# Mixer's output projection: three steps prepared during the last gates, its weight sums in the norm rows' room, and bank copies ahead of casts

## The chip, the cores and the metric

The kernel runs on one core of a Trainium2 chip. The metric is the device time of one execution in microseconds (us), median of several runs. The engines of the core run side by side, each in its own order: PE (TensorE: matmuls, and PEld its weight loads), DVE (VectorE), ACT (ScalarE), POOL (GpSimd) and SP (SyncE, which here issues all loads).

## The reference

Two layers of an encoder on a sequence of 512 tokens with 1024 channels, float32. Each layer has three sandwich-normalised blocks: a SwiGLU feed-forward (FFN1), a mixer, and a second feed-forward (FFN2).

```python
h = rms_norm(x, norm_pre[l, 0])
x = x + 0.5 * rms_norm(swiglu_ffn(h, ...), norm_post[l, 0])
h = rms_norm(x, norm_pre[l, 1])
m = hybrid_mixer(h, w_in[l], ..., w_branch[l], w_out[l])
x = x + rms_norm(m, norm_post[l, 1])
h = rms_norm(x, norm_pre[l, 2])
x = x + 0.5 * rms_norm(swiglu_ffn(h, ...), norm_post[l, 2])
```

The end of the mixer is what the change touches:

```python
branches = jnp.stack([sb_out, conv_out, gla_out], axis=2)      # each 512 x 512
branch_d = jnp.einsum('bsgw,gwd->bsgd', branches, w_branch)
gates = jax.nn.sigmoid(gate_logits.reshape(b, s, N_BRANCHES, D_MODEL))
merged = jnp.sum(gates * branch_d, axis=2)
return merged @ w_out
```

## The kernel before, in words

**Split products.** Every float32 operand of a matmul is split into a high part (a cast to the matmul's short float32 form, on ACT) and a low part (raw minus high, on DVE). Each product is three matmuls: high x high, high x low, low x high. A weight load of 128 x 1024 thus costs one cast (`whi`) and one subtraction (`wlo`). There are five buffers for such pairs, and three raw buffers of two halves each (`load_raw`), into which SP loads. Line 115/116 is the general `split`; lines 676, 677, 679 and 680 are the same for the output projections (`Down.parts`).

**Order.** A planner lays out each engine's instructions at build time. Instructions made with `pinned` (`keep_in_program_order`) stand behind everything that the program text has put on that engine before them; the others may be moved, and buffers of a kind are handed out as the plan goes. All matmuls are pinned.

**Gates.** `gates(g, src, done)` handles one branch g in eight steps d of 128 output channels. A step computes the gate logits (24 matmuls, bank `gate`), their sigmoid `gs` on ACT, the branch's projection (12 matmuls, bank `pb`), then the product of the two on DVE (line 1222) and the sum into `acc[d]` on POOL (line 1223). The branches come in the order 0, 2, 1; the last is the convolution's (`cv`), and only there `done` is given (`merge`). Before the change each step loads its own gate weights at its start.

**The output projection.** `merged @ w_out` has its first half (`acc[0..3]`, 512 of the 1024 inner channels) done as a block product with seven smaller products in place of eight (class `Down`, after Strassen and Winograd), and the other half (`acc[4..7]`) as ordinary products. A step p of the list `steps` is one product. `sums(p)` loads its weights and forms the sums of weights and of tokens on DVE (lines 642 and 662), `parts(p)` splits them into high and low parts, `product(p)` runs twelve matmuls into the banks oA, oB, oC or oD. `ahead()` does `sums` of the next step and `parts` of this one. The mixer has `PER` = 1 (one product per kind), the FFNs have 4. So the mixer's list is: steps 0 to 5 and 6 (the seven products), then steps 7 to 10 (`acc[4..7]`), whose matmuls run token block by token block in `out_proj`.

Four steps are prepared before the first product. Before the change one of them is prepared in gate step 6 of the last branch (`merge`), the others in `run` after the gates. `run` takes the room of the activations, xh, for the weight sums (`kept`), and xl for copies (`taps`) of banks that are used again. In the loop of `run` the preparation of a later step (`ahead`) comes first and the copy of a bank (line 720) after it.

**Norm rows.** Each block needs the norm's weight rows, one before and one after it, broadcast to 128 x 1024 (`load_g`, line 193, tag `g`, two buffers). An FFN loads them in `run` (`late`, after the products of kind 3); the mixer before its start.

Of the kernel before, what the change touches and what calls it, by code (L numbers as in the profile page):

```python
# [8 lines left out]
F32 = mybir.dt.float32  # L9
# [4 lines left out]
P = 128  # L14
D = 1024
S = 512
NT = S // P
KC = D // P
# [19 lines left out]
C_GQ, C_GK, C_GV, C_GR, C_LR, C_GATE = 2560, 2816, 3072, 3584, 4096, 4112  # L38
# [3 lines left out]
def kernel(  # L42
# [17 lines left out]
    gp = ctx.enter_context(tc.tile_pool(name="gp", bufs=2))  # L60
# [15 lines left out]
    def bank(n, tag="pb"):  # L76
        return psp.tile([P, 512], F32, tag=tag, name=n, bufs=BANKS[tag])
# [23 lines left out]
    def room(n, dt=F32R):  # L101
        cur[n] = resid.tile([P, KC, S], dt, tag=n, name=n)
        return cur[n]
# [47 lines left out]
    def proj_cols(w2d, c0, name, tag="pb"):  # L151
        wh, wl = load_cols(w2d, c0)
        ps = bank(name, tag)
        mm_cols(ps, wh, wl)
        return ps
# [140 lines left out]
    def mm_out(o, t, sh, sl, wh, wl, st=False, en=False):  # L296
        mm(o, sh[:, t], wh, start=st, stop=False, skip_group_check=True)
        mm(o, sh[:, t], wl, start=False, stop=False, skip_group_check=True)
        mm(o, sl[:, t], wh, start=False, stop=en, skip_group_check=True)
# [271 lines left out]
    class Down:  # L571
# [6 lines left out]
        def __init__(self, wd, hid, f0, np, middle, last):  # L578
            self.wd, self.hid = wd, hid
            self.F0, self.NP, self.PER = f0, np, np // 2  # L580
            self.MIDDLE, self.LAST = middle, last
            self.ready = {}
            self.s1 = None
            self.next = 0
            self.raw = {}
            self.plan()
# [36 lines left out]
        def load(self, p):  # L623
# [8 lines left out]
                                       self.wd[r0:r0 + 2 * P, HS[h]].rearrange("(k p) c -> p k c", p=P))]))  # L632
            self.raw[p] = raws

        def sums(self, p):

            self.load(p)
            j, c = self.steps[p]
            if j is None:
                return  # L640
            name, raws = self.ORDER[j][0], self.raw[p]
            tt = lambda o, a, b, op: pinned(nc.vector.tensor_tensor(o, a, b, op=op))
            kept = last = None
            if j >= 2:

                at = lambda n: self.kept[:, n:n + 2, :].rearrange("p k c -> p (k c)")
                last = at(2 * c)
                kept = at(2) if self.PER == 1 and j > 2 else last
            src = raws[0]
            if name == "S3":  # L650
                tt(kept, raws[0], raws[1], ALU.subtract)
                src = kept
            if name == "S2":
                for q, x in enumerate(self.of(p)):
                    tt(x, self.s1[c][:, q], x, ALU.add)
                tt(kept, last, raws[0], ALU.subtract)
                src = kept
            if name == "S4":
                for q, x in enumerate(self.of(p)):
                    tt(x, x, self.hid[self.F0 + 2 * c + q][:, self.R1], ALU.add)  # L660
            if name == "S1":
                pinned(nc.vector.scalar_tensor_tensor(src, kept, -1.0, raws[0], op0=ALU.mult, op1=ALU.subtract))
            if name == "A22":
                tt(src, kept, raws[0], ALU.add)
            self.raw[p] = src
# [43 lines left out]
        def run(self, late, order=("C0", "D0", "C1", "D1", "B0", "B1")):  # L709
            got = {n: bank("o" + n[0]) for n in order}  # L710
            c0, d0, c1, d1, b0, b1 = (got[n] for n in ("C0", "D0", "C1", "D1", "B0", "B1"))
            a0, a1 = (bank("oA", "pa") for i in range(2))
            self.banks = {"A": (a0, a1), "B": (b0, b1), "C": (c0, c1), "D": (d0, d1)}
            self.out = [[c0, d0], [c1, d1], [b0, a0], [b1, a1]]
            self.kept, taps = room("xh", F32), room("xl", F32)
            p1, p7, self.u2, self.u4 = ([taps[:, n + i, :] for i in range(2)] for n in (0, 2, 4, 6))

            def tap(o, b):
                for i in range(2):
                    pinned(nc.scalar.copy(o[i], self.banks[b][i]))  # L720

            while self.next < self.AHEAD:
                self.ahead()
            for p in range(self.end):
                j, c = self.steps[p]
                self.product(p)
                self.ahead()
                if c != self.PER - 1:
                    continue
                if j == 1:  # L730
                    tap(p1, "A")
                if j == 2:
                    tap(p7, "C")
                if j == 3:
                    tap(self.u2, "A")
                    late()
                if j == 5:
                    tap(self.u4, "A")
                    for i in range(2):
                        pinned(nc.vector.tensor_tensor(self.u4[i], p7[i], self.u4[i], op=ALU.subtract))  # L740

                    self.p1 = [slot("p1") for i in range(2)]
                    for i in range(2):
                        pinned(nc.scalar.copy(self.p1[i], p1[i]))
                    if not self.MIDDLE:

                        sh, sl, hi, lo = self.ready[self.end]
                        for i in range(2):
                            mm_out(self.out[i][1], slice(i * P, (i + 1) * P), sh, sl, hi[:, HS[1]], lo[:, HS[1]], st=True)
            while self.next < len(self.steps):  # L750
                self.ahead()
            rest = []
            for p in range(self.end, len(self.steps)):
                sh, sl, hi, lo = self.ready[p]
                rest.append((self.steps[p][1], (hi, lo), (sh, sl)))
            return self.out, rest, None if self.MIDDLE else self.LAST[0]
# [106 lines left out]
        return out_proj(wd, NF, None, TAIL, lambda i, b: finish(i, b, down.sum), upcoming, early, head)  # L863


    def mixer(l, wv, arrive, finish, upcoming, early):
        W = w_in[l]

        NR = TAPS + 3
# [136 lines left out]
        taps = []  # L1006
# [178 lines left out]

        acc = [None] * KC

        def gate_branch(g, d, src, wb):
            pg = proj_cols(W, C_GATE + g * D + d * P, "gate")
            sg = slot("gs", tag="s")  # L1190
            nc.scalar.activation(sg, pg, AF.Sigmoid)
            pb = bank("pb")
            wh, wl = wb
            for k in range(4):
                sh, sl = src[k]
                mm(pb, wh[:, k, :], sh, start=(k == 0), stop=False)
                mm(pb, wh[:, k, :], sl, start=False, stop=False)
                mm(pb, wl[:, k, :], sh, start=False, stop=(k == 3))
            return pb, sg
# [11 lines left out]
            return r  # L1211

        def gates(g, src, done):
            for d in range(0, KC, 2):
                wb = load_branch(g, d)
                for dd in (d, d + 1):
                    pb, sg = gate_branch(g, dd, src, wb[dd - d])
                    if acc[dd] is None:
                        acc[dd] = slot("acc", tag="q")
                        nc.vector.tensor_tensor(acc[dd], pb, sg, op=ALU.mult)  # L1220
                    else:
                        nc.vector.tensor_tensor(sg, pb, sg, op=ALU.mult)
                        nc.gpsimd.tensor_tensor(acc[dd], acc[dd], sg, op=ALU.add)
                    if done is not None:
                        done(dd)
                    yield
# [136 lines left out]
        def merge(d):  # L1363
            for n in range(2):
                down.sum_tokens(d, n)
            if d == KC - 2:
                down.ahead()

        for _ in gates(1, cv, merge):
            pass  # L1370
        head = down.run(lambda: None, ("B0", "B1", "C0", "C1", "D0", "D1"))
        return out_proj(w_out[l], KC, None, TAIL, lambda i, b: finish(i, b, down.sum), upcoming, early, head)


# [14 lines left out]
    weights = None  # L1389
    subs = [(l, s) for l in range(L) for s in range(3)]  # L1390
    for idx, (l, s) in enumerate(subs):
        norms = []

        def late():
            norms.append(load_g(norm_post[l, s]))
            if idx + 1 < len(subs):
                norms.append(load_g(norm_pre[subs[idx + 1][0], subs[idx + 1][1]]))

        if s == 1:
            late()  # L1400
        upcoming = []
        here, forms = forms, Forms() if s != 0 else None
        ahead = forms
# [19 lines left out]
        if s == 0:  # L1423
            weights = ffn(f1g[l], f1u[l], f1d[l], weights, here, arrive, finish, upcoming, early, late,
                          begin if idx == 0 else None)
        elif s == 1:
            weights = mixer(l, weights, arrive, finish, upcoming, early)
        else:
            weights = ffn(f2g[l], f2u[l], f2d[l], weights, here, arrive, finish, upcoming, early, late, None)
        arrive = upcoming  # L1430
# [29 lines left out]
```

## Time and profile before

| | |
|---|---|
| median of 3 runs | 2356.39 us (2355.69 to 2358.6) |
| profiled execution, its own time | 2358.0 us |
| its span, first to last instruction | 2356.3 us |
| mean granted TensorE clock | 0.994 |
| PE busy | 2315.5 us (98%) |
| DVE busy | 1887.7 us (80%) |
| ACT busy | 1240.8 us (53%) |
| POOL busy | 162.6 us (7%) |

The profile is one execution of the program. Its views used here are: the totals per engine; the chain of work that ended last (followed back from the last instruction to what released each step); windows, which give for a stretch of time the busy time and count of an engine, the granted TensorE clock and the load of the DMA engines; the timeline, one row per instruction with its start, its duration, engine, line, operation, output and inputs, and in brackets the idle time of the engine before it with what ended it; waits, which add such idle times up; and tiles, which show all instructions on one buffer name. Matmul durations overlap, since matmuls are pipelined; what counts is the distance from one start to the next.

### The profile page before, as it was taken

The page shows a single profiled execution, that of the slowest core. Times are in us where ns is not written, and L with a number is a line of the kernel's source. Part 1 is how long each engine was busy: PE and PEld are TensorE (multiplying, and loading weights), DVE is VectorE, ACT ScalarE, POOL GpSimd, SP SyncE. Part 2 cuts the span into 40 slices and gives each one's busy share as a digit, 9 for nine tenths or more (in the row PEclk, how much of TensorE's full clock was granted, in tenths as well). Part 3 has the DMA queues.
Part 4 walks back from the last instruction along what each step waited for, and adds up shares of the span by engine and source line. Part 5 has one row for each costly group of instructions (what it writes and reads, how often), then busy time and mean ns, then how long its engine had stood idle before and what let it go on. Part 6 is the DMA issues. An engine that isn't in the chain of part 4 may idle for free.

```text
span 2356.3 us, 36269 instructions
## 1 busy us (share of the span) xinstructions
PE 2315.5 (98%) x14048; PEld 2059.4 (87%) x14048; DVE 1887.7 (80%) x2819; ACT 1240.8 (53%) x2414; POOL 162.6 (7%) x277
## 2 busy tenths in 40 slices
PE   8999999999999899999999999999999998999998
PEld 7999888887888689998899998888878886999987
DVE  7888987859964688889888889877699637888897
ACT  5565656633322455556555566665433324655664
POOL 0000001201021000000000000022010210000000
PEclk9999999999999899999999999999999999999999
DMA  5333644141332323336423336532223323233363
GB/s 172 95 103 108 231 144 118 54 113 48 101 104 90 109 69 101 108 108 215 161 78 102 108 113 229 159 100 72 77 72 95 102 72 116 73 108 108 108 223 108
DMA packets 335965, 269.53 MB, mean 114 GB/s; under 512 B 12874, under 2 KB 285292, under 8 KB 335792
## 3 DMA queue, kind: packets, MB, share of 16 engines
q1 hardware_dynamic: 335792, 267.21, 37.4%
q8 instruction: 110, 1.80, 0.3%
q14 instruction: 63, 0.52, 0.1%
HBM read 265.07 MB, written 2.10 MB: 113 GB/s over the span
## 4 chain that ended last, share of the span: by engine, by line
PE 94%; DVE 3%; ACT 1%; issue 1%; DMA 0%; POOL 0%; SPq 0%; DVEq 0%; POOLq 0%; ACTq 0%
PE A L66 19%; PE gate L66 11%; PE oA L66 10%; PE C L66 9%; PE oC L66 6%; PE pb L66 5%; PE B L66 5%; PE oB L66 3%; PE pf L66 3%; PE gr L66 2%; PE pa L66 2%; PE q L66 2%; PE gv L66 2%; PE pv L66 2%; PE pgl L66 2%; PE k L66 2%
## 5 line engine op out<-in xcount | busy, mean ns | idle before, releaser
L457 DVE TENSOR_TENSOR wlo<-raw,whi 128x1024 fp32r<-128x1024 f32 (+1 forms) x304 | 331.2, 1089 | 108.4 <-ACT whi L455 107.6
L455 ACT CAST whi<-raw 128x512 fp32r<-128x512 f32 x532 | 315.3, 620 | 162.7 <-DVE raw L457 162.7
L115 ACT CAST whi<-raw 128x1024 fp32r<-128x1024 f32 (+1 forms) x162 | 168.1, 1044 | 323.1 <-PE gate L66 134.6
L116 DVE TENSOR_TENSOR wlo<-raw,whi 128x1024 fp32r<-128x1024 f32 (+1 forms) x162 | 203.6, 1266 | 134.0 <-ACT whi L115 129.8
L457 DVE TENSOR_TENSOR raw<-raw 128x512 f32<-128x512 f32 x304 | 209.3, 689 | 5.7
L66 PE MATMUL A<-xh,whi 128*128 128x256 f32 x608 | 172.5, 284 | 0.0
L66 PE MATMUL A<-xl,whi 128*128 128x256 f32 x608 | 172.0, 283 | 0.0
L66 PE MATMUL A<-xh,wlo 128*128 128x256 f32 x608 | 172.0, 283 | 0.0
L1042 DVE SCALAR_TENSOR_TENSOR y<-u,cw,y 128x511 f32<-128x511 f32 (+14 forms) x240 | 166.7, 756 | 0.0
L680 DVE TENSOR_TENSOR wlo<-raw,whi 128x1024 fp32r<-128x1024 f32 x122 | 149.3, 1223 | 18.4 <-ACT whi L677 18.4
L677 ACT CAST whi<-raw 128x1024 fp32r<-128x1024 f32 x122 | 128.4, 1052 | 64.8 <-issue 19.6
L66 PE MATMUL gate<-xh,wlo 128*128 128x512 f32 x384 | 152.3, 397 | 8.5 <-DVE wlo L116 8.5
L66 PE MATMUL gate<-xh,whi 128*128 128x512 f32 x384 | 153.4, 400 | 1.0 <-ACT whi L115 1.0
L66 PE MATMUL gate<-xl,whi 128*128 128x512 f32 x384 | 151.3, 394 | 0.0
L66 PE MATMUL oA<-whi,dh 128*128 128x512 f32 x352 | 139.2, 395 | 5.1 <-ACT xl L720 5.1
L66 PE MATMUL oA<-wlo,dh 128*128 128x512 f32 x352 | 140.0, 398 | 3.9 <-DVE wlo L680 3.9
L66 PE MATMUL oA<-whi,dl 128*128 128x512 f32 x352 | 138.7, 394 | 0.0
L268 POOL TENSOR_TENSOR rs<-ms,mhalf 128x1 f32<-128x1 f32 x44 | 25.1, 576 | 1453.6 <-DVE ms L266 1453.6
L455 ACT COPY cp<-A 128x256 f32<-128x256 f32 x228 | 84.4, 370 | 68.3 <-PE A L66 67.4
L66 PEld LDWEIGHTS A<-xl,whi 128*128 128x128 f32 x608 | 116.5, 192 | 0.2
L66 PEld LDWEIGHTS A<-xh,whi 128*128 128x128 f32 x608 | 116.4, 191 | 0.2
L66 PEld LDWEIGHTS A<-xh,wlo 128*128 128x128 f32 x608 | 116.5, 192 | 0.0
(324 smaller groups left out, 7088.9 us busy)
## 6 DMA issues: line engine op xcount, KB each, us to landing
raw<-in_ffn_w_down_dram SPq DMA_DIRECT2D x152, 512.0 KB, 4.6
raw<-in_w_in_dram SPq DMA_DIRECT2D x108, 512.0 KB, 4.5
raw<-in_ffn_w_gate_dram SPq DMA_DIRECT2D x152, 256.0 KB, 3.4
raw<-in_ffn_w_up_dram SPq DMA_DIRECT2D x152, 256.0 KB, 4.5
raw<-in_w_branch_dram SPq DMA_DIRECT2D x24, 512.0 KB, 3.7
raw<-in_w_out_dram SPq DMA_DIRECT2D x24, 512.0 KB, 4.7
raw<-in_ffn_w_gate_dram SPq DMA_DIRECT2D x12, 512.0 KB, 5.7
raw<-in_ffn_w_up_dram SPq DMA_DIRECT2D x12, 512.0 KB, 5.3
```

The costliest lines, as they stand in the source:

```text
L66: tc.keep_in_program_order(nc.tensor.matmul(*a, **k))
L115: pin(nc.scalar.copy(hi, src))
L116: pin(nc.vector.tensor_tensor(lo, src, hi.bitcast(F32), op=ALU.subtract))
L268: nc.gpsimd.tensor_tensor(self.rs, ms, mhalf[:, 0:1], op=ALU.pow)
L455: copy = lambda o, i: pin(nc.scalar.copy(o, i))
L457: tt = lambda o, a, b, op: pin(nc.vector.tensor_tensor(o, a, b, op=op))
L677: pinned(nc.scalar.copy(hi, src))
L680: pinned(nc.vector.tensor_tensor(lo, src, hi.bitcast(F32), op=ALU.subtract))
L1042: nc.vector.scalar_tensor_tensor(y[:, back:], u[:, :S - back], cw[:, c, j:j + 1], y[:, back:], op0=ALU.mult, op1=ALU.add)
```

## The change

1. In the last branch's `gates` the gate weights of step d + 1 are loaded before the matmuls of step d (`following`), those of step 0 before the branch's first weights.
2. `merge` prepares three steps of the output projection (`ahead` three times) in gate step 6, where it prepared one.
3. In the mixer the weight sums get two buffers of the tag `g` (`apart`) instead of the room of xh. The mixer's norm rows use the same two buffers, and are loaded by `late` after product 3 instead of before the mixer.
4. In the mixer's `run` the copies of banks, `late`, the early matmuls of step 7 and the difference for `u4` stand ahead of `ahead`; in the FFNs the order stays.

```diff
@@ class Down
-            self.s1 = None
+            self.s1 = self.apart = None
...
+        def place(self, n):
+            return self.kept[:, n:n + 2, :].rearrange("p k c -> p (k c)")
@@ Down.sums
-                at = lambda n: self.kept[:, n:n + 2, :].rearrange("p k c -> p (k c)")
-                last = at(2 * c)
-                kept = at(2) if self.PER == 1 and j > 2 else last
+                if self.PER == 1 and not self.apart:
+                    self.apart = [gp.tile([P, D], F32, tag="g", name="kept") for n in range(2)]
+                if self.PER > 1:
+                    last = kept = self.place(2 * c)
+                else:
+                    last, kept = self.apart[0], self.apart[min(j - 2, 1)]
@@ Down.run
-            self.kept, taps = room("xh", F32), room("xl", F32)
+            if self.PER > 1:
+                self.kept = room("xh", F32)
+            taps = room("xl", F32)
...
                 self.product(p)
-                self.ahead()
+                if self.PER > 1:
+                    self.ahead()
...
                         for i in range(2):
                             mm_out(self.out[i][1], slice(i * P, (i + 1) * P), sh, sl, hi[:, HS[1]], lo[:, HS[1]], st=True)
+                if self.PER == 1:
+
+                    self.ahead()
@@ mixer
-    def mixer(l, wv, arrive, finish, upcoming, early):
+    def mixer(l, wv, arrive, finish, upcoming, early, late):
...
-        def gate_branch(g, d, src, wb):
-            pg = proj_cols(W, C_GATE + g * D + d * P, "gate")
+        def gate_weights(g, d):
+            return load_cols(W, C_GATE + g * D + d * P)
+
+        def gate_branch(g, d, src, wb, w):
+            pg = bank("gate")
+            mm_cols(pg, *w)
...
         def gates(g, src, done):
+
+            early_ = done is not None
+            following = gate_weights(g, 0) if early_ else None
             for d in range(0, KC, 2):
                 wb = load_branch(g, d)
                 for dd in (d, d + 1):
-                    pb, sg = gate_branch(g, dd, src, wb[dd - d])
+                    w = following if early_ else gate_weights(g, dd)
+                    if early_ and dd + 1 < KC:
+                        following = gate_weights(g, dd + 1)
+                    pb, sg = gate_branch(g, dd, src, wb[dd - d], w)
...
             if d == KC - 2:
-                down.ahead()
+                for n in range(3):
+                    down.ahead()
...
-        head = down.run(lambda: None, ("B0", "B1", "C0", "C1", "D0", "D1"))
+        head = down.run(late, ("B0", "B1", "C0", "C1", "D0", "D1"))
@@ the layers' loop
-        if s == 1:
-            late()
...
-            weights = mixer(l, weights, arrive, finish, upcoming, early)
+            weights = mixer(l, weights, arrive, finish, upcoming, early, late)
```

## The prediction

> **What bounds the kernel now.** I read the page first: engine totals, the clock row, the chain.
>
> ```profile
> span 2356.3 us, 36269 instructions
> PE 2315.5 (98%) x14048; PEld 2059.4 (87%) x14048; DVE 1887.7 (80%) x2819; ACT 1240.8 (53%) x2414; POOL 162.6 (7%) x277
> PE 94%; DVE 3%; ACT 1%; issue 1%; DMA 0%; POOL 0%; SPq 0%; DVEq 0%; POOLq 0%; ACTq 0%
> ```
>
> TensorE (PE) sets the time: 94% of the chain lies on it, and it is idle for only about 41 us. The change adds and removes no matmul, so it can win only where PE waits or runs at a lower clock. Then I looked for those places with the chain and with windows around the mixer's end (columns of a window: length, PE busy and count, granted clock, DMA share, GB/s).
>
> ```profile
> 766.71 5.44 PE gate L66 x24
> 774.71:814.71 40.00, 31.74 (x110) 0.83 0.37 124
> 1943.62:1982.85 39.23, 29.68 (x110) 0.87 0.38 127
> 814.71:833.75 19.04, 19.04 (x85) 1.00 0.35 100
> ```
>
> The first row (chain of waits) is one undisturbed gate: 24 matmuls in 5.44 us, 0.2267 us each. The next two are the place that the change touches, once per layer: from where gate 7 of the last branch could start to the first matmul into bank oD. The program has 36 matmuls of gate 7 there and 72 of six block products, 108 in all (the window counts 110, with those on its edges). At 0.2267 us they need 24.48 us. They take 40.00 and 39.23, at a clock of 0.83 and 0.87; behind them it is 1.00. The loss is 15.52 + 14.75 = **30.27 us**, the most that this change can win there. The timeline of PE in both layers shows where it goes (start, us, and in brackets the idle time before it and who ended it):
>
> ```profile
> 774.48 0.39 PE L66 MATMUL pb<-brh,wlo 128*128 128x512 f32 x1
> 775.39 0.50 PE L66 MATMUL gate<-xh,whi 128*128 128x512 f32 x1 [0.52 <-ACT whi L115]
> 779.74 0.79 PE L66 MATMUL gate<-xh,wlo 128*128 128x512 f32 x1 [3.61 <-DVE wlo L116]
> 780.33 0.63 PE L66 MATMUL gate<-xh,whi 128*128 128x512 f32 x1
> 790.41 0.39 PE L66 MATMUL oB<-whi,dh 128*128 128x512 f32 x1
> 795.47 0.50 PE L66 MATMUL oA<-wlo,dh 128*128 128x512 f32 x1 [1.95 <-DVE wlo L680]
> 804.77 0.50 PE L66 MATMUL oA<-whi,dh 128*128 128x512 f32 x1 [2.19 <-ACT xl L720]
> 806.67 0.63 PE L66 MATMUL oA<-wlo,dh 128*128 128x512 f32 x1
> 814.71 0.39 PE L66 MATMUL oD<-whi,dh 128*128 128x512 f32 x1
> 1944.30 0.50 PE L66 MATMUL gate<-xh,whi 128*128 128x512 f32 x1 [0.52 <-ACT whi L115]
> 1948.64 0.80 PE L66 MATMUL gate<-xh,wlo 128*128 128x512 f32 x1 [3.61 <-DVE wlo L116]
> 1958.60 0.39 PE L66 MATMUL oB<-whi,dh 128*128 128x512 f32 x1
> 1963.66 0.50 PE L66 MATMUL oA<-wlo,dh 128*128 128x512 f32 x1 [1.95 <-DVE wlo L680]
> 1964.22 0.40 PE L66 MATMUL oA<-whi,dh 128*128 128x512 f32 x1
> 1967.27 0.50 PE L66 MATMUL oC<-wlo,dh 128*128 128x512 f32 x1 [0.58 <-DVE wlo L680]
> 1972.95 0.50 PE L66 MATMUL oA<-whi,dh 128*128 128x512 f32 x1 [2.89 <-ACT xl L720]
> ```
>
> Three stalls. Gate 7 waits for its own weights; without that wait oB would start at 774.71 + 36 x 0.2267 = 782.87 instead of 790.41 (7.54 us), in layer 1 at 1951.78 instead of 1958.60 (6.82). The second product waits for its low weight part, the fourth for a copy out of bank A. Together PE idles 8.27 us in layer 0 and 9.55 in layer 1; the other 7.3 and 5.2 of the loss are matmuls of 0.63 instead of 0.39 us, and restarts, behind the stalls (780.33, 806.67).
>
> **The change part by part.** The reason of the first stall stands in ACT's and DVE's order:
>
> ```profile
> 750.20 1.06 ACT L115 CAST whi<-raw 128x1024 fp32r<-128x1024 f32 x1 [1.17 <-PE pb L66]
> 772.25 0.60 ACT L1191 ACTIVATE gs<-gate 128x512 f32<-128x512 f32 x1 [7.56 <-PE gate L66]
> 772.74 0.70 ACT L676 CAST dh<-acc 128x256 fp32r<-128x256 f32 x2
> 773.35 1.05 ACT L677 CAST whi<-raw 128x1024 fp32r<-128x1024 f32 x1
> 774.29 1.04 ACT L115 CAST whi<-raw 128x1024 fp32r<-128x1024 f32 x1
> 774.98 0.69 DVE L1222 TENSOR_TENSOR gs<-pb,gs 128x512 f32<-128x512 f32 x1 [7.47 <-PE pb L66]
> 775.59 1.82 DVE L679 TENSOR_TENSOR dl<-acc,dh 128x256 fp32r<-128x256 f32 x2
> 775.81 1.31 POOL L1223 TENSOR_TENSOR acc<-acc,gs 128x512 f32<-128x512 f32 x1 [6.87 <-DVE gs L1222]
> 777.33 1.21 DVE L680 TENSOR_TENSOR wlo<-raw,whi 128x1024 fp32r<-128x1024 f32 x1
> 778.47 1.21 DVE L116 TENSOR_TENSOR wlo<-raw,whi 128x1024 fp32r<-128x1024 f32 x1
> 797.14 0.75 DVE L679 TENSOR_TENSOR dl<-acc,dh 128x256 fp32r<-128x256 f32 x2
> 804.14 1.07 ACT L720 COPY xl<-oA 128x512 f32<-128x512 f32 x2
> ```
>
> *Gate weights one gate ahead.* Nothing is added, two loads and splits change places. Gate 6's weights are cast at 750.20, 16 us before gate 6 starts. Gate 7's (L115 at 774.29) stand behind the pinned casts of step 0, and those behind gate 6's sigmoid. Loaded before gate 6, they come ahead of step 0, in the buffer that gate 4 leaves some 19 us before gate 7 starts (two gates of 8.16, and the 12 branch matmuls of gate 4, 2.72). The first stall goes: 7.54 + 6.82 us. What is late next is the products' preparation.
>
> *Three steps prepared in the last gate but one.* Same instructions, earlier. What held steps 1 and 2 back: the sums went into the room of xh, which gate 7 still reads.
>
> ```profile
> SPq L127 <- DVE xh L642: 75.1, 2, 37.9
> raw<-in_w_out_dram SPq DMA_DIRECT2D x24, 512.0 KB, 4.7
> DMA to landing us min/median/max: 3.5/4.5/5.5
> ```
>
> Even the load queue stood 37.9 us per layer for a sum in xh. With the sums in the norm rows' room, DVE runs on from 775.59 (from start to start: weight low 777.33 to 778.47, 1.14 us; a weight sum is of the same size, 1.13; a pair of token lows 0.67 of its 0.75, and 1.74 beside POOL's add). Step 0 is ready at 778.5, the sum and lows of step 1 at 781.4, the two token sums, the weight sum and lows of step 2 at 785.0. Then gate 7's multiply (0.61), and with sum and lows at about 3.0 us each, step 3 at 788.6, step 4 at 791.5, step 5 at 793.9 and step 6 at 795.7. PE, without a stall, starts product 0 at 782.87 and each next 12 x 0.2267 = 2.72 us later: 785.59, 788.31, 791.03, 793.75, 796.47; six matmuls into oD at 799.19, product 6 at 800.55. Every step is ready 2.2 us or more ahead, and this is the cover. POOL's add for gate 7 will stretch one low by 1.1 us (1.74 against 0.67), which the cover holds; without it the 1.1 us would stand on PE, once per layer. Raw weights: step 4's come into the raw buffer that step 0 and gate 7 shared, free at 778.5, and land 4.7 us later, at 783.3, for a sum at 785.6.
>
> On this stretching the Trainium skill ("Advanced Engine Details and Errata", Mode Summary) says that VectorE's second SBUF port is shared with GpSimd and that the two block each other. By it all of the moved DVE work that runs beside POOL's adds would slow down, at most 1.3 us per add; the two rows above (1.82 beside POOL, 0.75 without) agree, and the sum is the same by either.
>
> *Bank copies ahead of casts.* The fourth product waited for a copy (804.14) that stood behind casts waiting for DVE sums. Now the copy of bank A needs product 1's end (788.5) and is done at 789.5, for product 3 at 791.03. The reverse price: the casts of steps 5, 7 and 9 wait for copies. For step 9 that means: copy of A from 798.7 (its first half is whole 9 matmuls into product 5), a second pair of copies behind it (together 2.2 us), casts of steps 9 and 10 from 800.9, the low of step 10 ends at 805.45. PE reads it 10 matmuls and 8 weight parts into the first token, at 805.5. I take 0.4 us per layer for this, between 0 and 1.8 us (the whole chain of cast and low, 0.52 + 1.22, late).
>
> *Norm rows late.* Two 512 KB loads per layer leave the mixer's start and come behind product 3, their rooms free at 785 (low of step 2) and 790 (sum of step 5).
>
> ```profile
> SPq L193 <- DVE tn L272: 13.5, 2, 6.8
> 822.43 0.69 DVE L272 SCALAR_TENSOR_TENSOR tn<-xl,g 128x512 f32<-128x512 f32 x1
> ```
>
> At the mixer's start the queue no longer stands 6.8 us per layer; no PE wait lies there, so nothing is won. At the end they land by 790 + 5.5 = 795.5; first use is at 822.43 - 15.5 = 806.9: hidden by 11 us. Step 8's load may stand behind them on SP until 790 and land at 795 to 796.5; its cast is due at 796.5. Without cover it would hold up the copies of bank A behind it, about 1 us; counted in the 1.8.
>
> **Sum.** Against the profiled execution (2358.0 us, span 2356.3): -30.3 + 0.8 = -29.5, so 2328.5. The median, 2356.39, is 1.6 below that execution; I forecast 2356.4 - 29.5 = **2327** (likeliest case alone: 2324 to 2331).
>
> **The rivals.**
> - *Only the gate stall goes.* DVE has some 20 us of work from 775.6 to the low of step 6, in 25 us of PE work. If loads or POOL put it more than 2.2 us behind, waits come back at products 3 to 5, with the slow clock. Gain 7.54 + 6.82 = 14.4: **2342**. For it: the margins are one instruction wide. Against: they are worked from measured starts.
> - *The slow clock stays.* The part of the loss that is not idle time is 7.3 + 5.2 = 12.5 us. Were the slow runs periodic and not caused by the stalls, it would stay: 2327 + 12.5, **2339**. Against it: the windows before and after have clock 1.00. By the Trainium skill ("TensorE: Matmul & The Clock Gate", Why this matters for your kernels) only idle gaps over some 3 us throw the clock back. The trace differs: slow rows (806.67) follow a gap of 2.19 us, and in layer 1 the row at 1964.22 shows full speed behind one of 1.95; the measurement decides.
> - *Nothing changes.* The buffers decide: five for split weights, fourteen small slots, of which eight hold the last branch's splits until gate 7 ends. If steps 1 and 2 get theirs only then, the same work comes at the same time and gate 7's weights lie behind it: **2356**. Against: step 0 to 2 need six slots and gate 6's sigmoid one, and the fifteenth comes free at 777.1, with POOL's add.
> - *Slower: the gates starve.* One more gate's weights are held in the same five buffers. If in the last group each gate's cast starts only when the gate before leaves a buffer, cast and low (1.05 + 1.21) stand on PE, with 1.6 us of slow clock (8 matmuls): 3.9 us for each of 14 gates, 54 against 30: **2380**. It decides from 8 such gates on. Against: weights are cast 16 us ahead now, two gates.
>
> **How the numbers follow.** Forecast 0.70; gate stall only 0.13; slow clock stays 0.04; nothing 0.06; slower 0.07. 0.2% is 4.7 us, about what a measurement of this kernel can tell from no change. Faster: 0.87, same 0.06, slower 0.07. The range holds the forecast, the slow clock and the better half of the gate case: 2323 to 2342.
>
> **What would show it.** Windows like the two above: 108 matmuls in 24.5 to 26 us at clock 1.00; no wait of a gate for L116; the casts of steps 0 to 2 all behind gate 6's sigmoid and ahead of gate 7's; the xl copy of bank A ahead of step 5's cast; the norm rows' loads near product 3. I am wrong if products wait for L680 or L720 again, if gates 1 to 6 of the last group wait, or if the token stage starts with a wait.

## The result and the profile after

| | before | after |
|---|---|---|
| median of 4 runs | 2356.51 us (2355.69 to 2358.6) | 2327.96 us (2327.32 to 2329.25) |
| profiled execution, its own time | 2358.0 us | 2327.66 us |
| its span | 2356.3 us | 2325.9 us |
| mean granted TensorE clock | 0.994 | 0.999 |

The ratio is 0.9878, 95% interval [0.9861, 0.9895]: the changed kernel is 28.6 us faster, where 2327 us was forecast. The totals and the chain of the page after:

```profile
PE 2302.7 (99%) x14048; PEld 2052.4 (88%) x14048; DVE 1884.8 (81%) x2819; ACT 1240.1 (53%) x2414; POOL 176.8 (8%) x277
PE 96%; DVE 2%; ACT 1%; issue 0%; DMA 0%; POOL 0%; SPq 0%; DVEq 0%; POOLq 0%; ACTq 0%
```

PE does the same 14048 matmuls. Its busy time falls by 12.8 us (2315.5 to 2302.7), nearly all of it at the two places of the change, where the slow matmuls are gone (31.74 + 29.68 us before, twice 24.48 after). The rest of the 30.4 us of span is idle time. POOL is the one engine that got busier, by 14.2 us; more on that below.

Windows of the changed kernel, PE alone, for the place of the change in both layers (from gate 7's first matmul to the first into bank oD), and for a longer stretch that goes on into the ordinary products (columns: length, PE busy and count, granted clock, DMA share, GB/s):

```profile
773.31:797.79 24.48, 24.48 (x110) 1.00 0.62 215
1927.44:1951.92 24.48, 24.48 (x110) 1.00 0.63 215
773.31:825.93 52.62, 52.62 (x248) 1.00 0.46 150
1927.44:1980.06 52.62, 52.62 (x248) 1.00 0.47 150
```

The longer stretch in the kernel before, between the same matmuls:

```profile
774.71:842.71 68.00, 59.74 (x247) 0.90 0.32 101
1943.62:2010.85 67.23, 57.68 (x247) 0.92 0.32 102
```

The place took 40.00 and 39.23 us; now it takes 24.48 in both layers, which is 108 matmuls at 0.2267 us to the hundredth: nothing is left to win in it. Over the longer stretch the gain is 15.38 + 14.61 = 29.99 us.

The waits of PE over the whole changed kernel (columns: total us, times, longest us) are these five, and hold no product of the output projection and no gate of the last branch:

```profile
PE pt L71 <- DVE hn L223: 7.6, 1, 7.6
PE pf L66 <- ACT xh L115: 3.0, 3, 1.7
PE pt L71 <- DVE hn L290: 2.0, 3, 0.7
PE pf L66 <- DVE xl L116: 1.9, 4, 0.6
PE gate L66 <- DVE wlo L116: 1.3, 2, 0.6
```

The timeline shows the new order on ACT (start, us, and in brackets the idle time before it and who ended it). Gate 7's weights are cast at 754.24, 19 us before gate 7; gate 6's sigmoid at 770.85 is followed by the casts of steps 0, 1 and 2, all ahead of gate 7's sigmoid at 779.40; and the copy out of bank A (L728) precedes the next cast:

```profile
754.24 1.05 ACT L115 CAST whi<-raw 128x1024 fp32r<-128x1024 f32 x1 [4.38 <-PE gate L66]
770.85 0.60 ACT L1207 ACTIVATE gs<-gate 128x512 f32<-128x512 f32 x1 [7.56 <-PE gate L66]
771.94 1.05 ACT L683 CAST whi<-raw 128x1024 fp32r<-128x1024 f32 x1
773.50 1.05 ACT L683 CAST whi<-raw 128x1024 fp32r<-128x1024 f32 x1
778.39 1.05 ACT L683 CAST whi<-kept 128x1024 fp32r<-128x1024 f32 x1 [3.23 <-DVE kept L645]
779.40 0.60 ACT L1207 ACTIVATE gs<-gate 128x512 f32<-128x512 f32 x1
786.49 1.20 ACT L728 COPY xl<-oA 128x512 f32<-128x512 f32 x2
788.48 1.06 ACT L683 CAST whi<-raw 128x1024 fp32r<-128x1024 f32 x1 [0.27 <-ACT dh L682]
```

Laid matmul by matmul beside the kernel before, the profiled execution after is 1.40 us ahead before it reaches the place in layer 0 (0.9 of it from the program's first 18 us), gains 15.52 there, loses 0.74 between the layers and gains 14.75 in layer 1. The first figure and most of the third lie outside the place. The profiled execution before lay 1.5 us above its median and the one after 0.3 below, so 28.6 us between medians and 30.0 us in place are no contradiction. Why executions of the kernel before spread more (2353.8 to 2358.7 over all its runs) was not settled.

### The profile page after: what moved, and what is told of

It reads as the page before. It is cut to its first block, busy times and chain, and to the rows that moved or that the text cites. A ratio compares the mean times of both kernels' runs of the same rounds, so it can differ in the third digit from the quotient of the medians.

```text
span 2325.9 us, 36283 instructions
## 1 busy us (share of the span) xinstructions
PE 2302.7 (99%) x14048; PEld 2052.4 (88%) x14048; DVE 1884.8 (81%) x2819; ACT 1240.1 (53%) x2414; POOL 176.8 (8%) x277
## 4 chain that ended last, share of the span: by engine, by line
PE 96%; DVE 2%; ACT 1%; issue 0%; DMA 0%; POOL 0%; SPq 0%; DVEq 0%; POOLq 0%; ACTq 0%
PE A L66 19%; PE gate L66 11%; PE oA L66 10%; PE C L66 9%; PE oC L66 6%; PE pb L66 6%; PE B L66 5%; PE oB L66 3%; PE pf L66 3%; PE gr L66 2%; PE pa L66 2%; PE q L66 2%; PE gv L66 2%; PE pv L66 2%; PE pgl L66 2%; PE k L66 2%
## 5 line engine op out<-in xcount | busy, mean ns | idle before, releaser
L116 DVE TENSOR_TENSOR wlo<-raw,whi 128x1024 fp32r<-128x1024 f32 (+1 forms) x162 | 203.5, 1266 | 136.9 <-ACT whi L115 130.5
```

The costliest lines, as they stand in the source:

```text
L116: pin(nc.vector.tensor_tensor(lo, src, hi.bitcast(F32), op=ALU.subtract))
```

## The experiments

**The theory** is the prediction's: two things each cost PE time, gate 7's weights standing behind step 0 (14.4 us for both layers) and products that waited for their preparation (the rest), the slow clock being an effect of the stalls. **The rivals**: the weights alone would do it; the early preparation alone would do it, or the order of copies; or the slow clock comes by itself.

### The gate weights alone

The kernel before, with each gate's weights of the last branch loaded one gate ahead, and nothing else.

```
-            pg = proj_cols(W, C_GATE + g * D + d * P, "gate")
+            pg = bank("gate")
+            mm_cols(pg, *w)
...
+            early_ = done is not None
+            following = gate_weights(g, 0) if early_ else None
...
+                    w = following if early_ else gate_weights(g, dd)
+                    if early_ and dd + 1 < KC:
+                        following = gate_weights(g, dd + 1)
```

> The kernel before with one edit: the last branch's gate weights are loaded one gate ahead. Theory (the three stalls have three causes; gate 7 waited because its cast stood behind step 0's): gate 7 runs without a wait, products 1 and 3 still wait for the low part (about 2 us) and for the copy of bank A (2 to 3 us), slow matmuls behind them. Gain 7.5 + 6.8 us, so about 2342 us. Rival (the slow clock does not come from the stall): only the 4.1 us of idle time per layer go, 2348 us. Second rival (the wait only moves to the products, since DVE has the same work): 2352 us or more.

Measured: 2344.65 us, ratio 0.9946 [0.9931, 0.996] to the kernel before (2357.0 beside it). That is 12.4 us of the 28.6. The windows from gate 7 to bank oD, and PE's two longest waits there in layer 0:

```profile
773.99:806.50 32.51, 26.99 (x109) 0.95 0.45 153
1936.01:1966.94 30.93, 26.72 (x109) 0.94 0.43 142
```

```profile
PE oA L66 <- ACT xl L720: 3.0, 1, 3.0
PE oA L66 <- DVE wlo L680: 1.9, 1, 1.9
```

The gate's wait is gone and the products' waits stay: the copy of bank A now holds PE for 3.0 us in layer 0 (2.2 before) and 2.3 in layer 1 (2.9 before). The place takes 32.51 and 30.93 where 40.00 and 39.23 were: 7.5 + 8.3 us, against 14.4 for the two from the first stall. That this is more than the 12.4 us between medians is a matter of the executions profiled: this one (2342.36) was the fastest of its four, and it lies 15.6 us below the profiled one before.

### Everything but the gate weights

The changed kernel, with the gates' weights where they were:

```
-            early_ = done is not None
+            early_ = False
```

> The changed kernel without its first part: gate weights are again loaded at each gate's start, three steps are still prepared in gate step 6. Theory (order on ACT and DVE decides): gate 7's weights now stand behind three steps instead of one, its low part ends some 11 us after gate 7 could start (about 785 on the changed kernel's clock, against 774), slow clock behind it 2 us, the products run without a wait: 13 us lost per layer, about 2354 us. Rival (the parts add up, each with a share of its own): only the first stall's 14.4 us come back, 2342 us.

Measured: 2355.96 us over ten runs, ratio 0.9996 [0.9986, 1.0005]: no gain at all. PE's waits in layer 0, the low part of gate 7's weights in the timeline, and the window to oD:

```profile
PE gate L66 <- ACT whi L115: 6.9, 1, 6.9
PE gate L66 <- DVE wlo L116: 3.3, 1, 3.3
```

```profile
785.42 1.21 DVE L116 TENSOR_TENSOR wlo<-raw,whi 128x1024 fp32r<-128x1024 f32 x1
```

```profile
775.11:813.75 38.64, 28.45 (x109) 0.82 0.40 139
```

Gate 7's weights now stand behind three prepared steps in place of one, so the gate waits 10.2 us and the products none. The early preparation is paid nearly in full by the gate: the place takes 38.64 us where it took 40.00, and the medians show none of that. So the parts do not add: 12.4 us for the first alone, about nothing for the rest alone, 28.6 together.

### How many steps must be ready

The changed kernel with fewer steps prepared in gate step 6 (`for n in range(3)` becomes `range(1)` or `range(2)`).

> The changed kernel with one step prepared in gate step 6, as before, not three. Theory (DVE needs about 3 us per step, PE 2.72, so a step that starts behind gate 7's multiply is late): product 1 waits some 2 us, product 2 about 1, products 3 and 4 some tenths, slow clock 1.6 us once: about 5 us per layer, 2338 us. Rival (with the gate weights ahead and the copies first, preparing early adds nothing): 2329 us.

> The changed kernel with two steps prepared in gate step 6. Theory (DVE's 3 us per step against 2.72 on PE): step 2's low part ends at 787.3 on the changed kernel's clock, product 2 could start at 787.07: waits of some tenths at products 2 and 3, no slow clock, about 1 us per layer, 2330 us. Rival (the third step carries the gain): 2333 us.

Measured: 2337.93 us (ratio 0.9918 [0.9903, 0.9933]) with one step, 2331.14 (0.9877 to 0.9906) with two, 2327.96 with three. PE's waits in layer 0 with one step:

```profile
PE oA L66 <- DVE wlo L686: 1.9, 1, 1.9
PE oC L66 <- DVE wlo L686: 0.6, 1, 0.6
PE oD L66 <- DVE wlo L686: 0.2, 1, 0.2
```

The long stretch with one step, then with two (two kernels):

```profile
774.30:831.25 56.95, 54.19 (x247) 1.00 0.43 139
```

```profile
773.81:827.83 54.02, 53.80 (x248) 1.00 0.45 146
```

With one step the total came out as expected, but by other terms: I had put 1.6 us per layer down to the slow clock, and the clock stays at 1.00 behind a gap of 1.9 us. The waits shown add up to 2.7 us of the 4.33 that the stretch is longer than after (56.95 against 52.62); the rest lies in longer distances between matmuls at full clock. That the total fitted so well was luck. With two steps no wait of PE is left there that the profile records, and the stretch is still 1.4 us longer than after: the products start just as their low parts or the bank copies ahead of them end, with distances of 0.28 to 0.52 us between matmuls in place of 0.227. The third prepared step is what gives every later one a margin.

### Copies behind the casts again

In the loop of `run`, `self.ahead()` stands directly behind `self.product(p)` for this projection too, ahead of the bank copies, as before.

```
-                if self.PER > 1:
-                    self.ahead()
+                self.ahead()
...
-                if self.PER == 1:
-                    self.ahead()
```

> The changed kernel with the old order in the mixer's run: the preparation of a later step first, the copy of a bank after it. Theory (with three steps prepared, DVE no longer lags, so the casts ahead of the copy are quick): the copy of bank A for product 3 ends 0.4 us late, the other copies 0.2 to 0.3 us, about 1 us per layer: 2330 us. Rival (the order alone caused the wait of 2.2 and 2.9 us in the kernel before): that wait and its slow clock are back, 3.7 us per layer, 2335 us.

Measured: 2328.36 us, ratio 0.988 [0.9863, 0.9896], not to be told from the changed kernel. The trace shows what is left, the wait for the copy and the long stretch in layer 0:

```profile
PE oA L66 <- ACT xl L728: 0.4, 1, 0.4
```

```profile
773.61:826.75 53.14, 52.78 (x248) 1.00 0.46 149
```

The stretch is 0.5 us longer per layer (53.16 in layer 1). With three steps ready the order of casts and copies is worth 0.5 us per layer at most. With one step ready it looks worth more: the kernel with one step and copies first has no wait for a copy at all, where the one with the gate weights alone, one step and casts first waits 5.2 us for them in both layers. Those two also differ in the room of the sums and in the norm rows, so the order's own share is not shown.

### The sums in xh's room, and the norm rows

One kernel forms the weight sums in xh's room again, another also loads the norm rows at the mixer's start as before.

```
-                    self.apart = [gp.tile([P, D], F32, tag="g", name="kept") for n in range(2)]
+                    own = resid.tile([P, KC, S], F32, tag="xh", name="xh")
+                    self.apart = [own[:, 2 * n:2 * n + 2, :].rearrange("p k c -> p (k c)") for n in range(2)]
```

> The changed kernel with the weight sums in the room of xh, as before; the norm rows still come late. Theory (the room held DVE only as long as gate 7 reads xh, and that ends 2.7 us before the branch's last matmul): the first weight sum waits from 777 to 779 on DVE, the margin of 2.2 us and more takes most of it, at most 1 us per layer on PE: 2328 to 2330 us. Rival (the room was what kept steps 1 and 2 back): the low part of a product comes 2 us late again with slow clock behind it, 2336 us or more.

> The changed kernel with the sums in the room of xh and the norm rows loaded before the mixer, as before the change; gate weights, three steps and copies first stay. It is compared with the run that has the sums in xh and late norm rows (2331.4 us). Theory (neither the load queue's 6.8 us at the mixer's start nor the late loads lie on PE's path): the same within 1 us. Rival (late rows hold up step 8's load and its cast): 1 to 2 us per layer faster with early rows, 2328 us.

Measured: 2331.43 us (ratio 0.9892 [0.9878, 0.9907]) and 2331.44 (0.9892 [0.9877, 0.9907]). So where and when the norm rows load is worth nothing that can be measured, as predicted. The room is worth about 3.5 us, a little more than expected and at another place: not at products 1 and 2, whose sums I had thought would be late, but at step 7 (in bank oD). PE's wait and DVE's two in layer 0 with xh's room, and the long stretch:

```profile
PE oD L66 <- DVE wlo L687: 1.2, 1, 1.2
```

```profile
DVE xh L645 <- PE gate L66: 1.8, 1, 1.8
DVE dl L686 <- POOL acc L1246: 1.2, 1, 1.2
```

```profile
773.15:827.42 54.27, 53.08 (x248) 1.00 0.46 146
```

In the changed kernel step 7's low part ends 0.35 us before PE loads it, although DVE has waited 1.19 us for POOL (the rows are below), so without that wait the cover there would be about 1.5 us. Here DVE waits 1.8 us until gate 7 has read xh and 1.2 us for POOL, 1.4 more than this cover, and PE's next matmul starts 1.57 us after the one before it instead of 0.23.

### POOL's last add

The wait for POOL stands in the changed kernel too, though there the cover holds it (its row is below). Two kernels ask what it is: one does gate 7's sum into `acc` on DVE, the other gives gate 7's `gs` a buffer of another kind, so that nothing small waits for it.

```
-                        nc.gpsimd.tensor_tensor(acc[dd], acc[dd], sg, op=ALU.add)
+                        (nc.vector if early_ and dd == KC - 1 else nc.gpsimd).tensor_tensor(acc[dd], acc[dd], sg, op=ALU.add)
```

```
-            sg = slot("gs", tag="s")
+            sg = slot("gs", tag="t" if (g, d) == (1, KC - 1) else "s")
```

> The changed kernel with one instruction on another engine: gate 7's sum into acc on DVE instead of POOL. In the changed kernel POOL's sum took 9.30 us while DVE ran its row of two-input operations, and DVE waited 1.19 us for the small buffer that it held. Theory (that wait lies inside the cover): DVE's wait goes, DVE has 0.6 us more work, PE the same, 2328 us. Rival (the wait takes a part of PE's path): 1 us per layer faster, 2326 us. If the sum on POOL is long because of DVE and not for reasons of its own, no other POOL row may be long.

> The changed kernel with gate 7's gate values in a buffer of another kind (t), so that no later step waits for POOL to leave it. Question: why POOL's sum of gate 7 takes 9.30 us. Theory (POOL gets no turn while DVE runs two-input operations in an unbroken row; in the changed kernel it ends in the 1.19 us in which DVE waits for its buffer): DVE's row goes on without that pause to about 800 us on the changed kernel's clock, POOL's sum lasts 15 us or more, and step 10's cast, which reads the sum, may wait for it: step 10's low part up to 1.5 us late per layer, 2328 to 2331 us. Rival (POOL's time is its own, or set by the buffer): it stays at 9.3 us or falls to the usual 1.3 to 2.2 us, 2328 us.

Measured: 2327.19 us (ratio 0.9872 [0.9858, 0.9887]) and 2328.9 (0.988 [0.9864, 0.9897]); neither can be told from the changed kernel. POOL's add in layer 0 in the changed kernel, with the step that waits for it on DVE, and the same add with the other buffer:

```profile
784.47 9.30 POOL L1245 TENSOR_TENSOR acc<-acc,gs 128x512 f32<-128x512 f32 x1 [8.72 <-DVE gs L1244]
793.80 0.76 DVE L685 TENSOR_TENSOR dl<-acc,dh 128x256 fp32r<-128x256 f32 x2 [1.19 <-POOL acc L1245]
```

```profile
785.09 14.58 POOL L1245 TENSOR_TENSOR acc<-acc,gs 128x512 f32<-128x512 f32 x1 [8.72 <-DVE gs L1244]
798.55 2.28 DVE L749 TENSOR_TENSOR xl<-xl 128x512 f32<-128x512 f32 x2
```

In the changed kernel the add ends as DVE stops to wait for its buffer. With another buffer DVE does not stop, and the add goes on until it has lasted 14.58 us. A kernel with a fifteenth small buffer, which was to move DVE's wait to a later step, gave no time: its buffers need 5.59 KB per partition where 4.78 were left.

### Both margins at once, and a version with more

Sums in xh's room together with the last add on DVE:

> The changed kernel with the weight sums in the room of xh (2331.4 us alone) and gate 7's sum into acc on DVE. There step 7's low part was 1.2 us late in each layer, behind a wait of 1.8 us for xh and one of 1.2 us for POOL's buffer. Theory (both waits use up the same margin): without POOL's wait the low part is some 0.6 us late or not at all, about 2329 us. Rival (the wait for xh alone makes it late): 2331 us as before.

Measured: 2329.91 us, ratio 0.9885 [0.9869, 0.9902], between the changed kernel and the one with xh's room, and not to be told from either by the intervals. PE's recorded wait at oD falls from 1.2 to 0.2 us. The long stretch shows that this is not all:

```profile
774.01:827.79 53.78, 53.58 (x248) 1.00 0.45 147
```

The stretch is 0.49 us shorter than with xh's room alone (54.27), and still 1.16 longer than after (52.62). The two waits on DVE draw on one margin. POOL's wait alone fits into it; the wait for xh, here with 0.6 us of DVE's own time for the add, does not, and both together fit less.

Last, the changed kernel with the weights of all three branches one gate ahead (`early_ = True`) and the last add on DVE:

> The changed kernel with the gate weights of all three branches one gate ahead, and gate 7's sum into acc on DVE. Theory: the one wait for gate weights that is left (0.6 us at the first gate of each layer, with its restart about 1 us) goes too, nothing else changes: 2 us in all, 2325 to 2326 us. Rival (five weight buffers are too few where the state steps and the gates interleave): waits of gates for their casts in the first branch, 2330 us or more.

Measured: 2326.22 us (2325.38 to 2328.33), ratio 0.9869 [0.9854, 0.9883]. The two gate waits of 0.6 us at L116 are gone from PE's list and the place stays at its floor. It is the lowest median of all, but its interval overlaps that of the changed kernel: no measurable step further.

## Why the prediction was right, point by point

**The bound** (30.27 us to be won in place): 30.27 came, 15.52 and 14.75, since both windows now stand at their floor of 24.48.

**Gate weights ahead** (14.4 us): the first stall went as worked out, with the cast at 754.24. Alone it gave 12.4 us between medians, and 15.8 in the windows of an execution that was the fastest of its four. The rival "gate stall only" (2342) is what the kernel does without the other parts: 2344.65.

**Three steps early, the schedule on DVE**: all block products had their operands in time. The rows of the changed kernel, which runs 1.40 us ahead of the one before at this point (773.31 against 774.71):

```profile
782.51 1.21 DVE L686 TENSOR_TENSOR wlo<-kept,whi 128x1024 fp32r<-128x1024 f32 x1
786.05 1.21 DVE L686 TENSOR_TENSOR wlo<-kept,whi 128x1024 fp32r<-128x1024 f32 x1
794.48 1.22 DVE L686 TENSOR_TENSOR wlo<-raw,whi 128x1024 fp32r<-128x1024 f32 x1
796.22 1.22 DVE L686 TENSOR_TENSOR wlo<-raw,whi 128x1024 fp32r<-128x1024 f32 x1
797.79 0.19 PEld L66 LDWEIGHTS oD<-wlo,dh 128*128 128x128 f32 x1
802.86 1.22 DVE L686 TENSOR_TENSOR wlo<-raw,whi 128x1024 fp32r<-128x1024 f32 x1
```

Step 2's low ends at 783.72, on the prediction's scale 785.1 (785.0 predicted); step 3's at 787.26, 788.7 (788.6); step 6's at 795.70, 797.1 (795.7, so 1.4 late); step 10's at 804.08, 805.5 (805.45). Starting from measured starts and counting start to start, not durations, was precise to 0.1 us where nothing unforeseen came in.

The cover was read too large. "Every step is ready 2.2 us or more ahead" comes from a list that ends with step 6 and leaves out step 7, whose six matmuls into oD come before product 6. By the prediction's own terms (step 6 at 795.7, then a pair of token lows and a weight low, 0.6 and 1.14) step 7 is ready at about 797.4 for oD at 799.19, 1.8 us ahead. Measured, its low part ends at 797.44 (798.8 on the prediction's scale) and PE loads it at 797.79 (799.2): 0.35 us of cover were left. This is where the sums in xh's room made PE wait.

**The term that was wrong: POOL's add.** The step said that the add would stretch one low part by 1.1 us. It did not: DVE's lows took their usual 0.75 and the add took 9.30 us where its usual time is 1.29. What reached DVE was a wait of 1.19 us for the add's small buffer, at step 6. That wait happens to have the size of the stretch predicted, and the cover held it, at step 7 with 0.35 us to spare; so the sum came out by luck although this mechanism was wrong. The Trainium skill ("Advanced Engine Details and Errata", Mode Summary) says that GpSimd instructions and VectorE's two-port instructions block each other, since VectorE's second port is shared. The prediction left out the limit to two-port instructions, and no trace here tells an instruction's mode. The traces agree that the two engines interfere (9.30 us against 1.29), but not with the reading in the prediction that the price always lies on DVE.

**Copies ahead of casts** (0.4 us per layer lost behind oD): 0.14 was measured: from the first matmul into oD to the end of the longer stretch it is 52.62 - 24.48 = 28.14 us after, and 68.00 - 40.00 = 28.00 before (layer 1: 28.14 and 67.23 - 39.23 = 28.00). It lies where the prediction put it, at step 10: its low part ends at 804.08, and PE's weight load for it waits 0.26 us, until 804.13. The order itself is worth 0.5 us per layer at most once three steps are ready, by the experiment; the prediction named it as the cure of the 2.19 and 2.89 us stall, and the other parts cure nearly all of that without it.

**Norm rows late** (hidden): right. (The 37.9 us that the prediction gives per layer for the load queue's wait is the longer of two; its row says 75.1 us for both.) SP's queue took them where expected:

```profile
783.75 0.33 SPq L193 DMA_DIRECT2D g<-in_norm_post_dram  x1
784.12 0.43 SPq L127 DMA_DIRECT2D raw<-in_w_out_dram  x1
788.47 0.33 SPq L193 DMA_DIRECT2D g<-in_norm_pre_dram  x1
792.64 0.33 SPq L127 DMA_DIRECT2D raw<-in_w_out_dram  x1
```

Only the loads of steps 9 and 10 stand behind one or both of them, not step 8's as feared, and no PE wait follows.

**The rivals.** "The slow clock stays" is out: all four windows are at 1.00, and no experiment shows a slow clock in the place without a stall. "Nothing changes" is what happens without the gate weights (2355.96), through gate 7's cast and not through the buffers. "The gates starve" did not occur, even with all 24 gates of a layer ahead.

**The clock.** Stalls bring the slow clock here, but not each one. In the kernel before, gaps of 2.19 and 2.89 us were followed by matmuls of 0.63 us, and of its two gaps of 1.95 us only the one in layer 0 was. With the weights alone, the gap of 1.95 us in layer 0 passed at full speed and that of 3.0 us did not; in layer 1 a gap of 1.94 us was followed by the slow clock and a longer one of 2.27 us was not. With one step early, 1.95 us passed in both layers. The Trainium skill ("TensorE: Matmul & The Clock Gate", Why this matters for your kernels) puts the limit at idle gaps of about 3 us; in these traces gaps from 1.94 us on can cost the clock, and the same length need not.

The traces show what tells them apart: where the gap falls. By the clock records of the kernel before, its slow stretches at the two places begin at 778.96, 796.03, 806.27, 1946.32 and 1973.63 us and last 6.83, 3.41, 3.41, 6.83 and 3.41 us. The distances between these starts are 5, 3, 334 and 8 times 3.413 us, so the clock changes on a grid of 3.413 us. These are windows of that grid with the weights alone, two around the gap of 1.95 us in layer 0, then the one with the gap of 1.94 us in layer 1 and the next:

```profile
783.04:786.45 3.41, 2.22 (x10) 1.00 0.00 0
786.45:789.86 3.41, 2.65 (x12) 1.00 0.42 114
1946.99:1950.40 3.41, 1.47 (x7) 1.00 0.09 7
1950.40:1953.82 3.42, 3.42 (x10) 0.50 0.90 314
```

The first gap is spread over two windows, in each of which PE is busy for well over half of the time, and the clock stays. The second lies in one window, where PE is busy for 0.43 of it, and the next window runs at half speed. Over all the kernels here, between the first 12 us and the end of the program, every full-speed window with PE busy for 0.44 or less was followed by half speed and none with 0.51 or more; the two in between went one each way. This is read off the traces; no run moved a gap by itself. The expectation for one step early counted on the slow clock where none came.

## What to carry to other kernels

When one in-order queue prepares for two consumers, moving one consumer's preparation earlier only moves the stall unless the other's is moved too: here the parts alone gave 12.4 and about 0 us, and both together 28.6. Look first for the place's floor (matmul count times undisturbed spacing), then write out the preparing engine's schedule from start-to-start times, and compare the margin of every step, the last ones included, with the sum of all waits that could fall into it. Once enough steps are prepared ahead, the order among the rest hardly matters, and one step fewer already costs.

## What the runs showed of the hardware

I had not expected POOL's add to stretch so far. The same 128x512 addition on POOL, its 32 instances in the changed kernel (min, median, max in ns):

```profile
L1245 POOL TENSOR_TENSOR acc<-acc,gs x32: 1271/1288/9297, 656.8 to 1938.6; 128x512 f32<-128x512 f32 x32
```

In the kernel with the last add of each layer on DVE no add on POOL took more than 2.20 us. Gate 7's add took 9.30 us in the changed kernel, 11.11 with the sums in xh's room and 14.58 with the other buffer. In all of these DVE had a backlog of two-input operations when gate 7's multiply came, and the add ended only when DVE stopped to wait for it, or, with the other buffer, beside the pair of differences at 798.55, which took 2.28 us in place of 1.29. In the kernel before and with one or two steps prepared, DVE had been idle just before the multiply; there the add took 1.4 to 2.2 us, and instead one DVE operation was stretched by some 1.1 us (1.82 against 0.75 for a pair of lows). What decides whether POOL gets its turn beside a busy DVE stays open: no run varied the backlog by itself.
